# Decode's products in float32 on four column quarters, with three places for the raw weights and output tiles taken once

## The chip, the core and the metric

The kernel runs on one core of a Trainium2 chip. Its engines work at the same time and each in its own order: TensorE (PE, matrix products into PSUM; its weight loads are listed apart as PEld), VectorE (DVE), ScalarE (ACT), GpSimd (POOL) and SyncE (SP), whose queue here only starts transfers. Data are moved between device memory and the on-chip memory by 16 DMA engines, which are fed from queues of SP and of ACT. The metric is the device time of one execution in microseconds (us), the median of several; lower is better.

## The reference

One inference step of a hybrid decoder layer, for a prompt of 1024 tokens and for 8 samples of one token each, with the same weights, all in float32:

```python
x = layer_norm(ALPHA * x + 0.5 * swiglu(x, ffn1_wi, ffn1_wo), ...)
z = x @ w_in + b_in                    # q, k, v, o, i, f, B, C, h, merge gates a and b
h, C, n, m = mlstm_chunkwise(q, k, v, log_i, log_f, C0, n0, m0)
y_a = (head_norm(h) * sigmoid(z_o)) @ w_a
y_b = (z_B * short_conv(z_C * z_h)) @ w_b
x = layer_norm(ALPHA * x + (sigmoid(z_ga) * y_a + sigmoid(z_gb) * y_b) @ w_mix)
x = layer_norm(ALPHA * x + 0.5 * swiglu(x, ffn2_wi, ffn2_wo), ...)
x = layer_norm(ALPHA * x + sigmoid(x @ w_pg) * (p @ w_pp), ...)
```

For a sample, one step of the mLSTM, for each of 4 heads and 8 samples, is an update of a 256 x 256 state matrix and one product with the query:

```python
C_new = w_c * C + outer(k * exp(dec - m_new), v)
num = C_new^T q          # then divided by the normaliser and normed over the head
```

In the kernel this part is called decode: 32 matrices, each read from `state_C`, changed, multiplied with the query and written to `C_sample`.

## The kernel before

**Precision.** A large product in float32 is made from products in a reduced format (`float32r`): each operand is split into a high part (ACT copies and rounds it) and a low part (DVE subtracts), and three products, high x high, high x low, low x high, are added in PSUM. The helpers are `hilo` (L210 to L212), `put` within `wcomb` (L258, L259) for weights, and `product` (L429 to L434).

**Pairs.** The projection `z = x @ w_in` is worked in pairs of 128 columns (256 columns at once) by a scheme with seven products instead of eight (`pair`, L438 and after). A pair has 14 steps: seven combinations j of weights and inputs, each for two groups of tokens s (256 and 260 columns). A step is 4 x 3 matmuls. Snapshots of partial sums go to on-chip memory by ACT (L450, L457, L461, L465), and DVE adds them into the output tiles (L454, L469, L470, L474).

**Weights.** For a pair, `wraw` loads two halves of 512 KB each (L245, SP's queue) into two places and `wcomb` makes seven weight combinations from both: L267 (DVE) and L270 (DVE), L268 and L275 (POOL) are sums and differences. The combinations go to a ring of nine slots, so the preparation of the next pair runs while the present pair computes.

**The last twelve pairs.** `lin` (L1018 and after) is called twelve times: four pairs for the gate o (stored in blocks, `oscr`), four for the merge gate b (`bscr`) and four for a (`ascr`). ACT applies the sigmoid (L1025); SP's queue starts the stores (L949 for o, L1027 for a and b). In these twelve pairs `count["step"]` is 0: each pair takes its raw weights in the same two places, `praws[2:4]`, and makes its two output tiles anew on the same two places `psgs[0:2]`. The other places of both lists serve decode.

**Decode beside the pairs.** `beside` is a list of lists: after each step of a pair its first entry is taken off and what it holds is recorded at that point, behind the latest snapshot on ACT. 168 entries are made for the 168 steps of the twelve pairs. For matrix n, counted from step 9n/2: `dec_load` (transfer on ACT's queue, step +0), `dec_value` (the value row to all partitions, +4), `dec_update` (+7: ACT scales the matrix, L1187; DVE adds the outer product, L1189), `dec_split` for both halves of 128 rows (+7 and +9: `hilo`, and after the second half the store to `C_sample`), and `dec_product` for both halves (+12 and +14, L1203). A product has the query of one sample as stationary operand: 16 columns, the high and the low part of the query, each with zeros but in the sample's column, so the products of the 8 samples of a head add up in one PSUM bank `pn` (16 rows). After the last one DVE copies the bank (L1207), `dec_sum` adds high and low parts by a small matmul with `sel` (L1211), and `dec_norm` and `dec_end` finish the head. Three places hold matrices, two hold value rows, three hold split halves.

**Order.** The tile framework sets the semaphores and plans the order on each engine with a cost model; a tile that is made anew on a place waits until all accesses to the old one are over, and within one tile overlapping accesses are ordered. Each engine, and each transfer queue, takes its instructions in the planned order.

Of the kernel before, what the change touches and what calls it, by code (L numbers as in the profile page):

```python
# [9 lines left out]
R = mybir.dt.float32r  # L10
I32 = mybir.dt.int32
AF = mybir.ActivationFunctionType
OP = mybir.AluOpType
# [23 lines left out]
def F_(ap):  # L37
    return ap.bitcast(F32)
# [25 lines left out]
def layer_kernel(ctx: ExitStack, tc: tile.TileContext, I, O):  # L64
    nc = tc.nc
    V, S, G, T, DQ = nc.vector, nc.scalar, nc.gpsimd, nc.tensor, nc.sync
# [10 lines left out]
    def gen(i, dt=F32, n=NT):  # L77

        tag = f"a{i}" if isinstance(i, int) else i
        return sb.tile([128, 1024 if tag in WN else 4 * BM], dt, name=tag, tag=tag)[:, :1024 if tag in WN else n]  # L80
# [14 lines left out]
    def tmp(n=BM):  # L95
        return tmpp.tile([128, BM], F32, name="tmp", tag="tmp")[:, :n]
# [17 lines left out]
    ident = sb.tile([128, 128], F32, name="ident")  # L114
# [17 lines left out]
    def slot():  # L132
        s = ring["slots"][ring["i"] % len(ring["slots"])]
        ring["i"] += 1
        return gen(s, R)
# [27 lines left out]
    def wrow(w, rows, half, dst=None):  # L163

        t = [wload(w[r:r + 128, half * 512:(half + 1) * 512].rearrange("p (k n) -> p k n", n=128), 4, 128,
                   gen(dst[i], R) if dst else None) for i, r in enumerate(rows)]
        return [[(hi[:, j, :], lo[:, j, :]) for hi, lo in t] for j in range(4)]
# [42 lines left out]
    def hilo(dst, src):  # L210
        order_["hi"] = S.copy(dst[0], src).ins
        order_["lo"] = V.tensor_tensor(dst[1], src, F_(dst[0]), op=OP.subtract).ins  # L212
# [28 lines left out]
    def wraw(w, c0, slots):  # L241
        out = []
        for i in range(2):
            t = gen(slots[i])[:, :D].rearrange("p (k n) -> p k n", n=256)
            DQ.dma_start(t, w[i * 512:(i + 1) * 512, c0:c0 + 256].rearrange("(k p) n -> p k n", p=128))  # L245
            out.append(t)
        return out

    def wcomb(raws):

        lo_, up = raws
        g = lo_.shape[1]
        a11, a21, a12, a22 = lo_[:, :, 0:128], lo_[:, :, 128:256], up[:, :, 0:128], up[:, :, 128:256]

        def put(src):
            s = slot()
            hi, lo = (s[:, i * 512:i * 512 + g * 128].rearrange("p (k n) -> p k n", n=128) for i in range(2))
            S.copy(hi, src)  # L258
            V.tensor_tensor(lo, src, F_(hi), op=OP.subtract)  # L259
            return hi, lo  # L260

        def fresh():
            return rawp.tile([128, 512], F32, name="raw", tag="raw")[:, :g * 128].rearrange("p (k n) -> p k n", n=128)

        s1, s2, s3 = fresh(), fresh(), fresh()
        out = [put(a11)]
        V.tensor_tensor(s1, a21, a22, op=OP.add)  # L267
        G.tensor_tensor(s3, a11, a21, op=OP.subtract)  # L268
        out.append(put(a12))
        V.tensor_tensor(s2, s1, a11, op=OP.subtract)  # L270
        out.append(put(s2))
        out.append(put(a22))
        out.append(put(s1))
        s4 = fresh()
        G.tensor_tensor(s4, a12, s2, op=OP.subtract)  # L275
        out.append(put(s3))
        out.append(put(s4))
        return out
# [157 lines left out]
    beside = []  # L436
# [299 lines left out]
    w_in = I["w_in"][0]  # L736
    XP = x7()
    praws, psgs = [31, 32, 24, 25], [22, 23, 20, 21]
# [8 lines left out]
    vscr = tc.dram_tile([4, 8, 256], F32, name="vscr")  # L747
    count = {"sg": 0, "w": 0, "step": 1}

    def sg_pair():  # L750
        i = 2 * (count["sg"] % 2)
        count["sg"] += count["step"]
        return [gen(psgs[i + q]) for q in range(2)]

    def in_pair(c0):
        i = 2 * (count["w"] % 2)
        count["w"] += count["step"]
        return wcomb(wraw(w_in, c0, praws[i:i + 2]))


    nT = sb.tile([128, 2, 32], F32, name="nT")
# [22 lines left out]
    def sg(shape, name):  # L784
        return sb.tile(shape, F32, name=name)
# [192 lines left out]
    for m in range(8):  # L978
        DQ.dma_start(x2scr[m], rp[m])
    w0 = in_pair(CC0)  # L980
    for k in range(2):
        lin_store((qscr, kscr)[k], qk[k], 0, k)
# [140 lines left out]
    sgn = sg([8, 258], "sgn")  # L1123
    dn = sg([8, 4], "dn")
    dec = {}
    sel = sg([16, 8], "sel")
    PS = sb.tile([128, 128], R, name="ps_")

    def smp_load(i, t):
        DQ.dma_start(t[:, 0:64].rearrange("p (m b) -> p m b", b=8), smscr[i].rearrange("m p b -> p m b"))  # L1130
        return t[:, 0:64].rearrange("p (h t b) -> p h t b", h=4, t=2)
# [19 lines left out]
        V.tensor_copy(dn, pd[0:8, 0:4])  # L1151

    def dec_start():
        t = gen(psgs[2], R)
        dec["qd"] = [t[:, i * 256:i * 256 + 256].rearrange("p (t a b) -> p t a b", t=2, b=16) for i in range(2)]
        c0, c1 = gen(psgs[3]), gen(praws[1])
        dec["cd"] = [c0[:, 0:512], c0[:, 512:1024], c1[:, 0:512]]
        dec["vb"] = [c1[:, 512:768], c1[:, 768:1024]]
        u = gen(praws[0], R)
        dec["hl"] = [v.rearrange("p (i e) -> p i e", i=2) for v in (t[:, 512:1024], u[:, 0:512], u[:, 512:1024])]  # L1160
        q8 = smp_load(0, tmp())
        dec["q"] = [PS[:, 64 * i:64 * i + 64].rearrange("p (h t b) -> p h t b", h=4, t=2) for i in range(2)]
        hilo(dec["q"], q8)
        V.tensor_tensor(sel, ident[0:16, 0:8], ident[0:16, 8:16], op=OP.add)

    def dec_query(h):
        e8 = eye8.rearrange("p (a b) -> p a b", b=8)
        for dt in range(2):
            for i in range(2):
                x = F_(dec["q"][i][:, h, dt])  # L1170
                V.tensor_tensor(dec["qd"][h % 2][:, dt, :, 8 * i:8 * i + 8], x[:, None, :].to_broadcast([128, 8, 8]), e8,
                                op=OP.mult)

    def dec_load(n):
        h, s = divmod(n, 8)
        dec[n] = dec["cd"][n % 3].rearrange("p (t e) -> p t e", t=2)
        S.dma_start(dec[n], I["state_C"][0, s, h].rearrange("(t p) e -> p t e", p=128))
        if s == 0:
            dec_query(h)

    def dec_value(n):
        S.dma_start(dec["vb"][n % 2], bass.AP(tensor=vscr.tensor, offset=vscr.offset + n * 256, ap=[[0, 128], [1, 256]]))
# [5 lines left out]
        for dt in range(2):  # L1188
            V.scalar_tensor_tensor(cd[:, dt], vb, kws[:, h, dt, s:s + 1], cd[:, dt], op0=OP.mult, op1=OP.add)  # L1189

    def dec_split(n, dt):
        h, s = divmod(n, 8)
        hl = dec["hl"][(2 * n + dt) % 3]
        hilo((hl[:, 0], hl[:, 1]), dec[n][:, dt])
        if dt:
            S.dma_start(O["C_sample"][0, s, h].rearrange("(t p) e -> p t e", p=128), dec[n])

    def dec_product(n, dt):
        h, s = divmod(n, 8)
        if s + dt == 0:  # L1200
            dec["pn"] = psp.tile([128, 512], F32, name="pn", tag="pn", bufs=1)
        for i in range(2):
            T.matmul(dec["pn"][0:16, 0:256], dec["qd"][h % 2][:, dt, s], dec["hl"][(2 * n + dt) % 3][:, i],  # L1203
                     start=(s + dt + i == 0), stop=(s == 7 and dt == 1 and i == 1))
        if s + dt == 8:
            dec["both"] = tmp(256)[0:16]
            V.tensor_copy(dec["both"], dec["pn"][0:16, 0:256])  # L1207

    def dec_sum(h):
        ph = aux(256)  # L1210
# [32 lines left out]

    if count["sg"] % 2:
        psgs = psgs[2:] + psgs[:2]
    count.update(sg=0, w=1, step=0)
    dec_start()
    beside += [[] for _ in range(168)]
    for n in range(32):
        for f, late in ((dec_load, 0), (dec_value, 4), (dec_update, 7)):  # L1250
            beside[n * 9 // 2 + late].append(partial(f, n))
        for dt in range(2):
            beside[n * 9 // 2 + 7 + 2 * dt].append(partial(dec_split, n, dt))
            beside[n * 9 // 2 + 12 + 2 * dt].append(partial(dec_product, n, dt))
        if n % 8 == 7:
            for f, late in ((dec_sum, 20), (dec_norm, 23), (dec_end, 28)):
                beside[n * 9 // 2 + late].append(partial(f, n // 8))
# [27 lines left out]
    for i in (34, 29, 20, 21):  # L1285
        t = gen(i, R, 4 * BM).rearrange("p (i t e) -> p i t e", i=2, e=BM)[:, :, :, 0:258]
# [126 lines left out]
    def wa_in(t, m):  # L1413
        s = gen((18, 28, 23)[m % 3]).rearrange("p (d n) -> p d n", n=516)
        DQ.dma_start(s[:, 0], ascr[m][:, half_cols(t)])
        DQ.dma_start(s[:, 1], tbscr[m][:, half_cols(t)])
        return s, wcol(I["w_a"][0], m * 128)
# [60 lines left out]
    for m in range(0, 8, 2):  # L1478
        u = [wa_in(1, m + i) for i in range(2)]
# [17 lines left out]
    w = wrow(w_mix, rows, 0, r_[0:5] + [18])  # L1497
# [167 lines left out]
    def out_new(t=None):  # L1665
        k = count["o"]
        count["o"] += 1
        return obufs[k % 2] if t is None else t, wkb.rearrange("p a b c -> p (a b c)")[:, k % 2 * 28:k % 2 * 28 + 28]
# [109 lines left out]
    t = gen(21, R)  # L1778
# [14 lines left out]
    o, st = [t[:, 520:1032] for t in (a31, a32)], out_new()[1]  # L1793
# [36 lines left out]
```

## Time and profile before

| | |
|---|---|
| time, median of 3 runs | 2691.32 us (2690.53 to 2692.86) |
| the profiled execution | 2685.85 us, span 2684.0 us |
| matmul records of decode's products (L1203) | 128, from 1236.2 to 1457.7 us |
| small products of `dec_sum` (L1211) | 8 records, from 1294.8 to 1466.5 us |
| weight load of 16 columns for L1203 | 94 ns median |
| scaling of a state matrix on ACT (L1187) | 32 of 810 to 839 ns |
| DMA in the last twelve pairs (1220 to 1478 us) | 202 GB/s |
| DVE and ACT over the whole span | 70% and 48% busy |

A line of the profile has the engine, the line of the kernel, the operation, what it writes and reads by the program's names, sizes, and times. Matmul records overlap: one of 260 columns is listed with about 0.28 us, but the next one starts 0.12 us later; the distance of the starts is what a matmul costs PE. In a list of waits the three numbers are us in total, times, and the longest. A row of a window has its start and end, its length, and then the busy time and the count of PE, PEld, DVE, ACT and POOL, the granted clock of PE, the busy share of the DMA engines and GB/s. In brackets at the end of a timeline row stands the idle time before it and what ended it.

### The profile page before, as it was taken

Reading aid. Unit: us, or ns where it says so; the run is one execution under the profiler, and the core shown is the slowest. Engines: PE = TensorE matmul, PEld = TensorE weight load, DVE = VectorE, ACT = ScalarE, POOL = GpSimd, SP = SyncE. Lnnn points to the kernel's source line nnn. Section 1 sums busy time; section 2 is a strip of 40 time slices with the busy share of each in tenths; the row PEclk is TensorE's granted clock in tenths of the full one; section 3 lists DMA queues with packets and bytes.
Section 4 is the critical chain, followed back from the end, with each engine's and each line's share of the span. In section 5 each row is a group of like instructions: output and inputs, shape, how many; then the busy total and the mean of one; then the engine's idle time right before and its main releaser. Section 6 shows DMA issues by size and latency. Waiting matters only on the chain.

```text
span 2684.0 us, 56381 instructions
## 1 busy us (share of the span) xinstructions
PE 2638.3 (98%) x21775; PEld 2604.1 (97%) x21775; DVE 1871.4 (70%) x4124; ACT 1287.8 (48%) x2839; POOL 652.8 (24%) x648
## 2 busy tenths in 40 slices
PE   9999999999999999999999999999999999999998
PEld 9999999999999999999999999999999999999887
DVE  6755556997885756656666678658855555888887
ACT  5444446433554445446666555425544444543351
POOL 2222221112421111111111345323422222111454
PEclk9999999999999999999999999999999999999999
DMA  6333235432332434236657776821423323643211
GB/s 207 103 108 107 91 105 197 161 121 68 115 97 88 123 99 127 79 89 191 188 176 243 236 238 219 256 81 46 157 91 107 104 89 107 219 154 114 86 47 58
DMA packets 311924, 355.15 MB, mean 132 GB/s; under 512 B 28536, under 2 KB 246344, under 8 KB 311656
## 3 DMA queue, kind: packets, MB, share of 16 engines
q1 hardware_dynamic: 289336, 330.30, 38.7%
q10 hardware_dynamic: 22320, 21.26, 2.6%
q8 instruction: 170, 2.79, 0.4%
q14 instruction: 98, 0.80, 0.1%
HBM read 246.09 MB, written 105.42 MB: 131 GB/s over the span
## 4 chain that ended last, share of the span: by engine, by line
PE 79%; DVE 9%; DMA 5%; ACT 2%; issue 2%; POOL 1%; SPq 0%; ACTq 0%; DVEq 0%; POOLq 0%
PE mm L432 13%; PE mm L433 13%; PE mm L434 13%; PE aux L432 5%; PE aux L434 5%; PE aux L433 5%; PE mm L172 5%; PE mm L174 5%; PE mm L173 5%; PE pn L172 1%; PE pn L173 1%; PE pn L174 1%; DVE a L212 1%; DVE a L589 1%; DVE w L259 1%
## 5 line engine op out<-in xcount | busy, mean ns | idle before, releaser
L432 PE MATMUL mm<-a,w 128*128 128x260 f32 (+1 forms) x2313 | 654.9, 283 | 3.4 <-DVE a L612 2.5
L433 PE MATMUL mm<-a,w 128*128 128x260 f32 (+1 forms) x2313 | 651.0, 282 | 0.9 <-DVE a L212 0.9
L434 PE MATMUL mm<-a,w 128*128 128x260 f32 (+1 forms) x2313 | 649.9, 281 | 0.0
L432 PEld LDWEIGHTS mm<-a,w 128*128 128x128 f32 x2313 | 435.3, 188 | 9.0 <-issue 3.7
L433 PEld LDWEIGHTS mm<-a,w 128*128 128x128 f32 x2313 | 435.7, 188 | 1.5 <-DVE a L212 1.3
L434 PEld LDWEIGHTS mm<-a,w 128*128 128x128 f32 x2313 | 435.3, 188 | 0.1
L275 POOL TENSOR_TENSOR raw<-a,raw 128x512 f32<-128x512 f32 (+2 forms) x98 | 124.6, 1272 | 1149.1 <-issue 448.8
L259 DVE TENSOR_TENSOR w<-raw,w 128x512 fp32r<-128x512 f32 (+2 forms) x258 | 174.6, 678 | 189.5 <-ACT w L258 188.2
L432 PE MATMUL aux<-a,w 128*128 128x260 f32 (+1 forms) x1000 | 282.0, 282 | 1.8 <-DVE a L454 1.5
L433 PE MATMUL aux<-a,w 128*128 128x260 f32 (+1 forms) x1000 | 281.1, 281 | 0.0
L434 PE MATMUL aux<-a,w 128*128 128x260 f32 (+1 forms) x1000 | 281.1, 281 | 0.0
L432 PE MATMUL mm<-a,e 128*128 128x260 f32 (+1 forms) x785 | 222.5, 283 | 0.9 <-DVE a L612 0.6
L433 PE MATMUL mm<-a,e 128*128 128x260 f32 (+1 forms) x785 | 221.2, 282 | 0.7 <-DVE a L212 0.7
L434 PE MATMUL mm<-a,e 128*128 128x260 f32 (+1 forms) x785 | 220.8, 281 | 0.0
L174 PE MATMUL mm<-a,w 128*128 128x256 f32 (+3 forms) x739 | 208.0, 284 | 0.2 <-DVE w L149 0.2
L172 PE MATMUL mm<-a,w 128*128 128x260 f32 (+4 forms) x695 | 198.0, 286 | 3.2 <-DVE a L647 1.7
L173 PE MATMUL mm<-a,w 128*128 128x260 f32 (+4 forms) x695 | 197.0, 285 | 0.0
L258 ACT CAST w<-a 128x512 fp32r<-128x512 f32 (+2 forms) x200 | 117.2, 587 | 161.5 <-PE mm L434 95.3
L432 PEld LDWEIGHTS aux<-a,w 128*128 128x128 f32 x1000 | 188.2, 188 | 2.9 <-DVE a L454 2.0
L434 PEld LDWEIGHTS aux<-a,w 128*128 128x128 f32 x1000 | 188.2, 188 | 0.0
L433 PEld LDWEIGHTS aux<-a,w 128*128 128x128 f32 x1000 | 188.2, 188 | 0.0
L258 ACT CAST w<-raw 128x512 fp32r<-128x512 f32 (+2 forms) x258 | 152.2, 591 | 65.6 <-PE aux L434 21.6
(546 smaller groups left out, 7726.1 us busy)
## 6 DMA issues: line engine op xcount, KB each, us to landing
a<-in_ffn_wi_dram SPq DMA_DIRECT2D x80, 512.0 KB
a<-in_w_in_dram SPq DMA_DIRECT2D x68, 512.0 KB
a<-hsum SPq DMA_DIRECT2D x119, 258.0 KB
hsum<-a SPq DMA_DIRECT2D x68, 258.0 KB
a<-in_ffn_wo_dram SPq DMA_DIRECT2D x40, 384.0 KB
a<-in_state_C_dram ACTq DMA_DIRECT2D x32, 256.0 KB
out_dram<-a ACTq DMA_DIRECT2D x32, 256.0 KB
raw<-in_w_b_dram SPq DMA_DIRECT2D x32, 256.0 KB
```

The source lines that it names most:

```text
L172: T.matmul(ps, wh, xh, start=(i == 0), stop=False)
L173: T.matmul(ps, wh, xl, start=False, stop=False)
L174: last = T.matmul(ps, wl, xh, start=False, stop=(i == n - 1))
L212: order_["lo"] = V.tensor_tensor(dst[1], src, F_(dst[0]), op=OP.subtract).ins
L258: S.copy(hi, src)
L259: V.tensor_tensor(lo, src, F_(hi), op=OP.subtract)
L275: G.tensor_tensor(s4, a12, s2, op=OP.subtract)
L432: T.matmul(ps, wh, xh, start=start and kp == 0, stop=False, skip_group_check=True)
L433: T.matmul(ps, wh, xl, start=False, stop=False, skip_group_check=True)
L434: T.matmul(ps, wl, xh, start=False, stop=stop and kp == len(xs) - 1, skip_group_check=True)
L589: V.tensor_tensor(lo, F_(lo), F_(hi), op=OP.subtract)
```

## The change

Decode's products are made in float32, without a split: `dec_split` and its `hilo` are gone, and `dec_store` only stores. Products come for two matrices at once (after odd n): four matmuls, for two samples and two halves of rows, each into its own quarter of the columns of the array (`tile_position=(0, 32 * j)`) and so into its own 32 rows of `pn`. The stationary operand has 32 columns per sample, of which 8 are used and the rest is zero from a memset. `pn` is copied with all 128 rows, and `sel` adds the four quarters. Four places hold state matrices. The value row is loaded two steps earlier, the store stands at +10, the product at +10 counted from the odd matrix. The two output tiles are made once for all twelve pairs (`fixed`), and the raw weights rotate over three places `praws[1:4]`; `praws[0]` holds the value rows and the stationary operand.

```diff
+    fixed = []
+
     def sg_pair():
+        if count["step"] == 0:
+            return fixed
         i = 2 * (count["sg"] % 2)
-        count["sg"] += count["step"]
+        count["sg"] += 1
         return [gen(psgs[i + q]) for q in range(2)]

     def in_pair(c0):
-        i = 2 * (count["w"] % 2)
-        count["w"] += count["step"]
-        return wcomb(wraw(w_in, c0, praws[i:i + 2]))
+        i = count["w"]
+        count["w"] += 1
+        return wcomb(wraw(w_in, c0, [praws[1 + (2 * i + q) % 3] for q in range(2)] if count["step"] == 0 else
+                          praws[i % 2 * 2:i % 2 * 2 + 2]))
...
     def dec_start():
...
+        c0, c1, c2 = gen(psgs[2]), gen(psgs[3]), gen(praws[0])
+        dec["cd"] = [c[:, o:o + 512] for c in (c0, c1) for o in (0, 512)]
+        dec["vb"] = [c2[:, 0:256], c2[:, 256:512]]
+        dec["qd"] = c2[:, 512:1024].rearrange("p (t a b) -> p t a b", t=2, b=32)
+        G.memset(dec["qd"], 0.0)
+        q8 = smp_load(0, F_(PS))
+        V.tensor_tensor(sel, ident[:, 0:8], ident[:, 32:40], op=OP.add)
+        for j in (64, 96):
+            V.tensor_tensor(sel, sel, ident[:, j:j + 8], op=OP.add)
+        dec["q"] = q8

     def dec_query(h):
         e8 = eye8.rearrange("p (a b) -> p a b", b=8)
         for dt in range(2):
-            for i in range(2):
-                x = F_(dec["q"][i][:, h, dt])
-                V.tensor_tensor(dec["qd"][h % 2][:, dt, :, 8 * i:8 * i + 8], x[:, None, :].to_broadcast([128, 8, 8]), e8,
-                                op=OP.mult)
+            V.tensor_tensor(dec["qd"][:, dt, :, 0:8], dec["q"][:, h, dt][:, None, :].to_broadcast([128, 8, 8]), e8,
+                            op=OP.mult)
...
-    def dec_split(n, dt):
+    def dec_store(n):
         h, s = divmod(n, 8)
-        hl = dec["hl"][(2 * n + dt) % 3]
-        hilo((hl[:, 0], hl[:, 1]), dec[n][:, dt])
-        if dt:
-            S.dma_start(O["C_sample"][0, s, h].rearrange("(t p) e -> p t e", p=128), dec[n])
-
-    def dec_product(n, dt):
+        S.dma_start(O["C_sample"][0, s, h].rearrange("(t p) e -> p t e", p=128), dec[n])
+
+    def dec_product(n):
         h, s = divmod(n, 8)
-        if s + dt == 0:
+        if s == 0:
             dec["pn"] = psp.tile([128, 512], F32, name="pn", tag="pn", bufs=1)
         for i in range(2):
-            T.matmul(dec["pn"][0:16, 0:256], dec["qd"][h % 2][:, dt, s], dec["hl"][(2 * n + dt) % 3][:, i],
-                     start=(s + dt + i == 0), stop=(s == 7 and dt == 1 and i == 1))
-        if s + dt == 8:
-            dec["both"] = tmp(256)[0:16]
-            V.tensor_copy(dec["both"], dec["pn"][0:16, 0:256])
+            for dt in range(2):
+                j = 2 * i + dt
+                T.matmul(dec["pn"][32 * j:32 * j + 32, 0:256], dec["qd"][:, dt, s + i], dec[n + i][:, dt],
+                         start=(s == 0), stop=(s == 6), tile_position=(0, 32 * j), skip_group_check=True)
+        if s == 6:
+            dec["both"] = tmp(256)
+            V.tensor_copy(dec["both"], dec["pn"][:, 0:256])
...
-    count.update(sg=0, w=1, step=0)
+    fixed.extend(gen(psgs[q]) for q in range(2))
+    count.update(w=0, step=0)
     dec_start()
     beside += [[] for _ in range(168)]
     for n in range(32):
-        for f, late in ((dec_load, 0), (dec_value, 4), (dec_update, 7)):
+        for f, late in ((dec_load, 0), (dec_value, 2), (dec_update, 7), (dec_store, 10)):
             beside[n * 9 // 2 + late].append(partial(f, n))
-        for dt in range(2):
-            beside[n * 9 // 2 + 7 + 2 * dt].append(partial(dec_split, n, dt))
-            beside[n * 9 // 2 + 12 + 2 * dt].append(partial(dec_product, n, dt))
+        if n % 2:
+            beside[n * 9 // 2 + 10].append(partial(dec_product, n - 1))
+        if n % 8 == 0:
+            beside[n * 9 // 2 + 8].append(partial(dec_query, n // 8))
```

More of the change, by code (lines that the diff above doesn't have):

```diff
@@ L1125, in layer_kernel @@
     dec = {}
-    sel = sg([16, 8], "sel")
+    sel = sg([128, 8], "sel")
     PS = sb.tile([128, 128], R, name="ps_")
@@ L1153, in dec_start @@
     def dec_start():
[L1154 to L1164, printed above, removed]
+        c0, c1, c2 = gen(psgs[2]), gen(psgs[3]), gen(praws[0])
[8 more added lines that the diff above has]
+        dec["q"] = q8
     def dec_query(h):
@@ L1168, in dec_query @@
         for dt in range(2):
-            for i in range(2):
-                x = F_(dec["q"][i][:, h, dt])
-                V.tensor_tensor(dec["qd"][h % 2][:, dt, :, 8 * i:8 * i + 8], x[:, None, :].to_broadcast([128, 8, 8]), e8,
-                                op=OP.mult)
+            V.tensor_tensor(dec["qd"][:, dt, :, 0:8], dec["q"][:, h, dt][:, None, :].to_broadcast([128, 8, 8]), e8,
+                            op=OP.mult)
     def dec_load(n):
         h, s = divmod(n, 8)
-        dec[n] = dec["cd"][n % 3].rearrange("p (t e) -> p t e", t=2)
+        dec[n] = dec["cd"][n % 4].rearrange("p (t e) -> p t e", t=2)
         S.dma_start(dec[n], I["state_C"][0, s, h].rearrange("(t p) e -> p t e", p=128))
-        if s == 0:
-            dec_query(h)
     def dec_value(n):
```

## The prediction

> **What bounds the kernel now.** I read the page's head first, then the chain that ended last, then one window over the stage that the change touches, from the first to the last of the twelve pairs that have decode beside them.
>
> ```profile
> span 2684.0 us, 56381 instructions
> PE 2638.3 (98%) x21775; PEld 2604.1 (97%) x21775; DVE 1871.4 (70%) x4124; ACT 1287.8 (48%) x2839; POOL 652.8 (24%) x648
> ...
> PE 79%; DVE 9%; DMA 5%; ACT 2%; issue 2%; POOL 1%; SPq 0%; ACTq 0%; DVEq 0%; POOLq 0%
> ```
>
> ```profile
> 1220.00:1478.50 258.50, 252.22 (x2078) 243.54 (x2076) 172.20 (x408) 166.34 (x379) 31.27 (x25) 1.00 0.67 202
> 1240.00:1260.00 20.00, 20.00 (x171) 19.77 (x170) 16.00 (x33) 13.73 (x32) 2.70 (x2) 1.00 0.79 215
> ```
>
> TensorE (PE) bounds the whole and this stage too; its clock is full (1.00). A full 20 us holds 171 matmuls, 0.117 us each, so a step (12 matmuls) lasts 1.4 us. The 2078 records of the stage would fill 243 us of the 258.5: at most 15 us are lost, and that still holds restarts, a few slower float32 products and missing records. DVE stands at 67% and ACT at 64%: neither is the bound, but both work in order, so a wait at their head can reach PE. The waits of PE in this stage, and of DVE:
>
> ```profile
> PE pn L1203 <- DVE tmp L1207: 1.8, 1, 1.8
> PE aux L432 <- DVE a L454: 1.8, 3, 1.1
> PE pn L1203 <- DVE a L212: 0.9, 1, 0.9
> PE mm L432 <- DVE a L470: 0.8, 3, 0.4
> PE aux L432 <- DVE tmp L212: 0.6, 1, 0.6
> PE pn L1203 <- ACT a L211: 0.3, 1, 0.3
> ```
>
> ```profile
> DVE raw L267 <- DMA a<-in_w_in_dram: 11.7, 7, 2.6
> DVE a L1189 <- DMA a<-vscr: 11.0, 6, 3.7
> ...
> DVE a L454 <- DMA bscr<-a: 5.9, 3, 3.3
> DVE a L454 <- DMA oscr<-a: 5.7, 2, 3.1
> ...
> DVE a L454 <- DMA sm<-st: 3.8, 1, 3.8
> DVE a L454 <- DMA ascr<-a: 3.1, 2, 1.9
> ```
>
> PE always waits for a DVE or ACT result, but DVE itself waits for transfers: raw weights (L267), the value row of decode (L1189), and the store that still reads the output tile (L454). The largest PE wait shows the link: an addition held up by a transfer, and the copy of decode's sum (L1207) queued behind it, for which PE waits 1.8 us.
>
> ```profile
> 1287.47 0.42 DVE L454 TENSOR_TENSOR a<-sreg,aux 128x256 f32<-128x256 f32 x1 [3.84 <-DMA sm<-st]
> ...
> 1289.41 0.41 DVE L1207 COPY tmp<-pn 16x256 f32<-16x256 f32 x1
> ```
>
> A wait costs PE more than its listed length:
>
> ```profile
> 1226.46 0.28 PE L432 MATMUL mm<-a,e 128*128 128x260 f32 x1
> 1227.81 0.39 PE L432 MATMUL aux<-a,w 128*128 128x260 f32 x1 [1.07 <-DVE a L454]
> 1228.04 0.29 PE L433 MATMUL aux<-a,w 128*128 128x260 f32 x1
> ```
>
> From 1226.46 to 1228.04 stand 1.58 us for two matmuls that need 0.24: 1.34 lost, 0.27 more than listed.
>
> **The change, part by part.**
>
> **Waits.** Output tiles taken once: now every pair takes its two tiles anew and its first addition waits for all readers of the old ones, stores included; with the tile kept, only readers of the same columns count, and block 0's store is the oldest. Raw weights over three places: a pair's second half can be loaded when the previous pair's first half has been read, about half a preparation earlier than now. The value row is asked for five steps ahead of its use (late 2 against 7) instead of three: 7.1 us instead of 4.3, so of the six waits only the 3.7 keeps a remainder (0.9). Decode's matrices get four places instead of three. So the causes of five rows of PE's list go; they are 1.8+1.8+0.9+0.8+0.3 = 5.6 us in nine waits, with 9 x 0.27 = 2.4 of restarts 8.0 us. The sixth (0.6, behind the value transposes of the pair before) stays. What else could be late: the product now comes three steps (4.3 us) after the update of its second matrix, the update takes 0.8 us on ACT and two DVE operations, and PE's whole queue of pair matmuls stands behind a late product; the store issue on ACT also follows the update by three steps, with the casts of the weights behind it. I take 85% of 8.0, **-6.8 us**; bounds 0 (the same lateness moved) and -8.0.
>
> **Casts.** The hi/lo splits of 64 half matrices go:
>
> ```profile
> L212 DVE TENSOR_TENSOR a<-a,a 128x256 fp32r<-128x256 f32 (+1 forms) x72 | 36.6, 521 | 5.9 <-ACT a L211 5.7
> L211 ACT CAST a<-a 128x256 fp32r<-128x256 f32 (+1 forms) x72 | 30.7, 430 | 23.7 <-DVE a L1189 21.7 <-DMA a<-yscr 0.9 <-PE pn L1203 0.6
> ```
>
> 64 of 72 are decode's: 27 us of ACT and 33 of DVE within 258. They lie beside PE, so they count nothing themselves; they are a reason to believe that the waits go. The new extras are small and beside PE too: one POOL memset (POOL is busy 31 of 258.5 us), two more additions for `sel`, and half as many query multiplications. Traffic is the same: each state matrix, value row and weight is moved once, as now; only the issue places change. SP's queue:
>
> ```profile
> SPq L245 <- POOL raw L275: 30.0, 9, 4.7
> ```
>
> A weight load waiting for its place blocks the output stores behind it; a third place shortens that.
>
> **Products.** This is the large unknown. Now there are 128 reduced-precision products of 16 columns (32 matrices, two halves of rows, two parts each), of which this row groups 84:
>
> ```profile
> L1203 PE MATMUL pn<-a,a x84: 275/279/290, 1239.2 to 1454.6; 128*16 128x256 f32 x84
> ```
>
> ```profile
> 1412.89 0.40 PE L1203 MATMUL pn<-a,a 128*16 128x256 f32 x2
> 1413.13 0.28 PE L432 MATMUL mm<-a,w 128*128 128x260 f32 x1
> ```
>
> Two take 0.24 us, 0.12 each, without any gap around them: 128 x 0.12 = 15.4 us. Afterwards there are 64 float32 products in 16 groups of four. Float32 products of the same length exist:
>
> ```profile
> 2523.21 0.28 PE L172 MATMUL mm<-a,w 128*128 128x256 f32 x1
> 2523.33 0.59 PE L407 MATMUL aux<-sreg,onesm 128*128 128x256 f32 x2
> 2523.57 0.47 PE L173 MATMUL mm<-a,w 128*128 128x256 f32 x1
> 2523.87 0.28 PE L174 MATMUL mm<-a,w 128*128 128x256 f32 x1
> ```
>
> ```profile
> 1294.60 0.28 PE L434 MATMUL mm<-a,w 128*128 128x260 f32 x1
> 1294.81 0.59 PE L1211 MATMUL aux<-tmp,sel 16*8 16x256 f32 x2
> 1295.33 0.39 PE L432 MATMUL mm<-a,w 128*128 128x256 f32 x1
> 1295.56 0.28 PE L433 MATMUL mm<-a,w 128*128 128x256 f32 x1
> ```
>
> One float32 matmul of the program is two records (two halves). From 2523.21 to 2523.87 are 0.66 us with two ordinary matmuls, which leaves 0.42, 0.21 a half. With a small stationary operand (L1211) the same sum gives 0.96 - 0.24 = 0.72: 0.30 more, as gaps before, after and one matmul later. I charge these 0.30 to a group as the price of going to a part of the array and back. What four quarters do side by side no row shows. Bounds: all eight halves one behind the other, 8 x 0.21 + 0.30 = 1.98 us a group, 31.7 in all, +16.3; or the four quarters wholly side by side, 2 x 0.21 + 0.30 = 0.72, 11.5 in all, -3.9. Every record of this trace starts in program order, and the two halves of a quarter are neighbours in it; the second half must follow the first in the same quarter, and the next quarter's first half can start only beside it. That makes five slots, 5 x 0.21 + 0.30 = 1.35 us, 21.6 in all, **+6.2 us**. It is also the middle of the bounds (2, 5, 8), so I take it, although the nearest rows (halves of undivided products, one behind the other) lean to eight.
>
> The Trainium skill, "TensorE: Matmul & The Clock Gate", Part 3, says that matmuls on different quarters overlap but start and end strictly in program order, and gives 2.38 times for three column tiles. The order agrees with the starts here; no run before the change shows the overlap. An estimate from that factor (3.2 for four quarters) would make a group 1.68 / 3.2 + 0.30 = 0.83 us and the sum -2.2 instead of +6.2. The skill's "TensorEngine Tiling (Array Packing)", Key Properties, speaks against the change: every change of tiling mode drains the engine. The gaps around L1211 agree; without any such charge (16 x 0.30 = 4.8) the sum would be +1.4 instead of +6.2.
>
> The sum: +6.2 - 6.8 = -0.6 us, against the profiled execution's 2685.85 us (span 2684.0 plus 1.85 around it). The median of the runs is 2691.32, 5.5 us above this execution; I put the difference on the median: **2690.7 us**.
>
> **Rivals.**
>
> *Quarters wholly side by side* (both halves of each run in its quarter without holding up the next): -3.9 - 6.8 = -10.7, 2680.6 us, faster. For it: the quarters share neither columns nor output partitions. Against it: the program order of the halves. The Trainium skill's "TensorEngine Tiling (Array Packing)", Key Properties, says that tiles run independently, which would give this case.
>
> *One behind the other* (slower): the place is the group of L1203's successor, eight halves of 0.21 us with PE's queue behind them: +16.3 - 6.8 = +9.5, 2700.8 us. For it: all float32 rows here follow one another. It decides from 16 groups costing more than 15.4 + 6.8 + 5.4 = 27.6 us, 1.73 us each. Faster would need under 15.4 + 6.8 - 5.4 = 16.8, 1.05 each.
>
> *The waits stay* (the kept tile still waits as a whole, or a product waits for its update in place of the waits removed), with five slots: only a third of 8.0 goes, +6.2 - 2.7 = +3.5, 2694.8 us. For it: the shorter way from update to product, and a DVE that was up to 3.8 us late; against it: DVE and ACT lose work and each cause is met by a place more.
>
> **How the numbers follow.** About 0.2%, 5.4 us, is what a measurement of this kernel can tell from no change. Five slots with waits gone 0.45 (of it 0.08 faster, 0.35 same, 0.02 slower, by 3 us either way for the order that the planner makes anew); side by side 0.22, faster; one behind the other 0.18 (0.16 slower, 0.02 same); waits stay 0.15 (0.08 same, 0.07 slower). Together faster 0.30, same 0.45, slower 0.25. The range reaches to both other cases, 2679 to 2702: outside it lie parts of "side by side" with all waits gone and of "one behind the other" with few gone (down to 16.3 above the median with none), some 0.16. The forecast alone would be 2686 to 2695.
>
> **What would show it.** The eight records of a group and the start of the pair matmul after the next: 1.35 us longer than without the group says five slots, 0.72 side by side, 1.98 in a row. DVE's waits on transfers at L454 and at the weight sum should fall from 18.5 and 11.7 us to under 5 together, that on the value row to about 1; PE's list should keep the 0.6 and under 1.5 more. A PE wait of the new product for the update would show the third rival. I would be wrong also if the planner, which orders anew with other costs, put work of the next stage differently, or if the clock fell below 1.00 in the groups.

## The result, and the profile after

The changed kernel takes 2675.08 us in the median (2672.63 to 2676.36, 4 runs) against 2692.09 us for the kernel before beside it (2690.53 to 2694.49): ratio 0.9935, interval 0.9918 to 0.9952. The forecast was 2690.7 us with a range of 2679 to 2702: the time lies below it. In later jobs the ratio was 0.9942 (0.9929 to 0.9955) and 0.9948 (0.9934 to 0.9962). The changed kernel stays within 2672 and 2678 us in all of them; the kernel before moves between 2682 and 2699 from one execution and one job to another.

The head of the page after, and the chain that ended last:

```profile
span 2674.6 us, 56234 instructions
...
PE 2635.3 (99%) x21775; PEld 2597.2 (97%) x21775; DVE 1840.7 (69%) x4053; ACT 1272.1 (48%) x2774; POOL 650.9 (24%) x649
...
PE 85%; DVE 7%; DMA 4%; issue 2%; ACT 2%; POOL 1%; SPq 0%; DVEq 0%; ACTq 0%; POOLq 0%
```

PE is as busy as before in a shorter span, and the share of DVE and DMA in the chain fell from 14% to 11%. Where the time went is read best between two products that both kernels have, one before the first of the twelve pairs (`dec_dot`) and one behind the last (keys and queries of chunk 0). These rows give their first and last starts, first in the kernel before:

```profile
L1150 PE MATMUL aux<-ones,cbuf x16: 163/163/170, 1199.9 to 1200.3; 128*8 128x1 f32 x16
...
L1319 PE MATMUL aux<-a,a x128: 272/275/377, 1478.8 to 1687.4; 128*128 128x128 f32 x128
```

and after:

```profile
L1155 PE MATMUL aux<-ones,cbuf x16: 163/163/170, 1203.0 to 1203.4; 128*8 128x1 f32 x16
...
L1320 PE MATMUL aux<-a,a x128: 272/275/377, 1470.2 to 1678.9; 128*128 128x128 f32 x128
```

From the first start of the one to the first start of the other (called the stage below) 278.9 us became 267.2: 11.7 less. Behind it the products of L1319 and L1320 take 208.6 and 208.7 us, and ahead of it PE has the same matmuls in the same order in both. They took 3.1 us longer in this profile of the changed kernel (1199.9 to 1203.0), so the span fell by only 9.4 us, from 2684.0 to 2674.6, while the stage fell by 11.7. Three profiles of the kernel before give 278.9, 281.3 and 275.8 us for the stage, three of the changed one 267.2, 267.2 and 267.1.

All that is left of PE's waits after the change, and then of DVE's waits for transfers at the three lines of the prediction, both from 1220 to 1478.5 us:

```profile
PE mm L172 <- ACT w L1333: 0.2, 1, 0.2
```

```profile
DVE a L1189 <- DMA a<-vscr: 2.5, 4, 1.4
```

PE waits for nothing of the twelve pairs any more. At the weight sum (L267) and at the additions (L454) no wait for a transfer is left; the value row keeps 2.5 us, where the prediction had about 1. One group of float32 products, then the records of the same group that run between 1248.79 and 1248.84 us, and those that run between 1249.25 and 1249.35:

```profile
1248.58 0.28 PE L434 MATMUL mm<-a,w 128*128 128x260 f32 x1
1248.79 0.64 PE L1202 MATMUL pn<-a,a 128*32 128x256 f32 x8
1249.36 0.39 PE L432 MATMUL mm<-a,w 128*128 128x256 f32 x1
1249.58 0.28 PE L433 MATMUL mm<-a,w 128*128 128x256 f32 x1
```

```profile
1248.79 0.42 PE L1202 MATMUL pn<-a,a 128*32 128x256 f32 x4
```

```profile
1249.03 0.40 PE L1202 MATMUL pn<-a,a 128*32 128x256 f32 x4
```

By 1248.84 four of the eight records have begun, 50 ns after the first; the other four begin together from 1249.03, 0.24 us after the first. The trace has a sign of which they are: the semaphore increments that `one_quarter` below has on its second and fourth record, the second halves of its first two products, stand here on the fifth and sixth. So the first halves of the four products start first and then the second halves. The eight are through, to the next start, in 0.57 us, where the two halves of a single L1211 took 0.52. By the sum of the prediction the group costs 1.00 (from 1248.58 to 1249.58) - 0.24 = 0.76 us: the four quarters run side by side.

### The profile page after: what moved, and what is told of

Its sections match the earlier page's. It is cut to its first block, busy times and chain, and to the rows that moved or that the text cites. A ratio compares the mean times of both kernels' runs of the same rounds, so it can differ in the third digit from the quotient of the medians.

```text
span 2674.6 us, 56234 instructions
## 1 busy us (share of the span) xinstructions
PE 2635.3 (99%) x21775; PEld 2597.2 (97%) x21775; DVE 1840.7 (69%) x4053; ACT 1272.1 (48%) x2774; POOL 650.9 (24%) x649
## 4 chain that ended last, share of the span: by engine, by line
PE 85%; DVE 7%; DMA 4%; issue 2%; ACT 2%; POOL 1%; SPq 0%; DVEq 0%; ACTq 0%; POOLq 0%
PE mm L432 15%; PE mm L433 14%; PE mm L434 14%; PE aux L432 6%; PE aux L434 6%; PE aux L433 6%; PE mm L172 5%; PE mm L174 5%; PE mm L173 5%; PE pn L172 1%; PE pn L174 1%; PE pn L173 1%; DVE a L212 1%; DVE a L589 1%; DVE a L612 1%
```

## The experiments

**Both kernels again, the parts, and the whole.** `before_again` and `before_third` are the kernel before, `after_again` and `after_third` the changed one, without an edit. The three edits on waits can each be undone alone:

```diff
 # A: output tiles made anew
-            return fixed
+            return [gen(psgs[q]) for q in range(2)]
 # B: raw weights in two places
-        return wcomb(wraw(w_in, c0, [praws[1 + (2 * i + q) % 3] for q in range(2)] if count["step"] == 0 else
+        return wcomb(wraw(w_in, c0, praws[2:4] if count["step"] == 0 else
 # C: value row three steps ahead instead of five
-        for f, late in ((dec_load, 0), (dec_value, 2), (dec_update, 7), (dec_store, 10)):
+        for f, late in ((dec_load, 0), (dec_value, 4), (dec_update, 7), (dec_store, 10)):
```

`products_alone` is the changed kernel with A, B and C; `kept_tiles_alone` is the kernel before with `fixed` taken over from the change.

> The unchanged kernel of before, for its profile on the chip on which the others run. Stage: from the products of dec_dot to the first product of keys and queries of chunk 0; 278.9 us before, 267.2 after the change, 11.7 less, while the medians differ by 17. Theory 1 (the stage is all that the change touches): the stage is again 277 to 281 us, and what is over 11.7 us lies outside the stage and is the difference of two executions. Theory 2 (the first profile of before was a lucky one): the stage itself is 283 us or more, with more waits of PE in it. Ratio 1.000 +- 0.002.

> The changed kernel once more, beside the kernel before on the same chip. Theory 1: stage 266 to 269 us, everything outside it as in the kernel before of the same chip within 2 us, ratio 0.9945 to 0.996 (11.7 us and a bit). Theory 2: ratio 0.993 to 0.994 again (17 us) because before loses more in the stage than its first profile showed.

> The changed kernel with the three edits on waits undone: output tiles made anew, raw weights in the same two places each pair, the value row at +4. Float32 quarters, no splits and four places for matrices remain. Theory 1 (products are worth 3 us, waits are cured by the kept tiles, the third place and the earlier value row): 16 groups of 0.76 us, stage 273 to 276 us, ratio 0.998 to 0.999, DVE still waits 10 us or more for transfers at L454. Theory 2 (the work taken from ACT and DVE is what cured the waits): stage 267 to 270 us, ratio 0.994 to 0.996, no wait of PE in the stage.

> The kernel before with one edit: the two output tiles are made once for the twelve pairs. Theory 1: DVE's waits for stores at L454 (18.5 us) go, with them PE's waits on L454 and on L1207 (3.6 us listed, 4.7 with restarts): stage 273 to 276 us, ratio 0.998 to 0.999. Theory 2 (cast work is what delays): the waits move to the weight sum and the value row, stage 277 to 280 us, ratio 0.9995 to 1.0005.

Measured: `before_again` 0.9999 (0.999 to 1.0009), stage 281.3 us; `after_again` 0.9942 (0.9929 to 0.9955), stage 267.2; `products_alone` 1.000 (0.9991 to 1.001), stage 280.6; `kept_tiles_alone` 0.997 (0.9959 to 0.9981), stage 273.5. The first two lie between theories 1 and 2, so they don't decide. The third is met by neither theory: the new products with less work on DVE and ACT are worth nothing without the edits on waits. Kept tiles alone, without the products, are worth 8 us in the medians and 5 in the stage (from 278.7, the mean of the three profiles of before). In `products_alone` PE waits as in the kernel before, and also at the new product, for the update just ahead of it (and then DVE's longest wait):

```profile
PE mm L432 <- DVE a L470: 3.4, 4, 1.9
PE pn L1202 <- DVE a L1189: 2.3, 3, 1.5
PE aux L432 <- DVE a L454: 1.2, 2, 0.7
```

```profile
DVE raw L267 <- DMA a<-in_w_in_dram: 28.8, 8, 5.7
```

In `before_again` the longest wait shows what such a wait costs beyond its length. The timeline of PE, and windows of 4 us (behind the busy times: granted clock, DMA share, GB/s):

```profile
1311.44 0.39 PE L1203 MATMUL pn<-a,a 128*16 128x256 f32 x2
1313.64 0.38 PE L432 MATMUL aux<-a,e 128*128 128x256 f32 x1 [1.81 <-DVE a L454]
...
1314.45 0.42 PE L434 MATMUL aux<-a,e 128*128 128x256 f32 x1
1314.66 0.41 PE L432 MATMUL aux<-a,e 128*128 128x256 f32 x1
```

```profile
1312.00:1316.00 4.00, 2.36 (x13) 2.36 (x14) 2.80 (x10) 2.22 (x6) 0.00 (x0) 0.77 0.15 42
1316.00:1320.00 4.00, 4.00 (x29) 3.95 (x29) 2.34 (x7) 2.47 (x8) 1.36 (x1) 0.80 0.49 122
1320.00:1324.00 4.00, 4.00 (x36) 3.95 (x35) 2.09 (x5) 2.77 (x6) 1.29 (x1) 1.00 0.77 240
```

Soon after the wait the matmuls start 0.21 us apart instead of 0.12 and the granted clock falls. From 1314.10 to 1317.45, 16 matmuls took 3.35 us instead of 1.9: 1.4 us on top of the wait. The wait of the same length in the first profile (1.80 us at 1289.97) was not followed by this, so one and the same wait costs 2.0 or 3.4 us. The 280.6 us of `products_alone` hold such a stretch too, after its wait of 1.9 us at L470:

```profile
1256.00:1260.00 4.00, 3.67 (x19) 3.67 (x20) 3.42 (x8) 3.10 (x7) 0.00 (x0) 0.63 0.46 131
```

**The law of the quarters.**

```diff
-                T.matmul(dec["pn"][32 * j:32 * j + 32, 0:256], dec["qd"][:, dt, s + i], dec[n + i][:, dt],
-                         start=(s == 0), stop=(s == 6), tile_position=(0, 32 * j), skip_group_check=True)
+                k = j % 1        # two_quarters: j % 2
+                T.matmul(dec["pn"][32 * k:32 * k + 32, 0:256], dec["qd"][:, dt, s + i], dec[n + i][:, dt],
+                         start=(s == 0 and j < 1), stop=(s == 6 and j >= 3), tile_position=(0, 32 * k), ...)
```

> The changed kernel with all four float32 products of a group in the first quarter of the columns, one sum instead of four; everything else as changed. Law A (each quarter works for itself, a group costs its fullest quarter's halves x 0.21 us and 0.34 for going there and back): 8 x 0.21 + 0.34 = 2.02 us a group against 0.76, 16 x 1.26 = 20.2 us more, stage 287 us, some 2697 us, ratio 1.002. Law B (halves overlap only with the next product, in program order): the same 2.02 here, as nothing can overlap. If the time grows by less than 15 us, float32 halves in one quarter overlap too, and the quarters are not the reason.

> The changed kernel with the four products of a group in two quarters, in turn (0, 1, 0, 1). Law A: 4 x 0.21 + 0.34 = 1.18 us a group, 16 x 0.42 = 6.7 us more than changed, stage 274 us, ratio 0.9967. Law B: five slots, 5 x 0.21 + 0.34 = 1.39 us, 10.1 us more, stage 277 us, ratio 0.998.

A group of `one_quarter`, then one of `two_quarters`:

```profile
1247.21 0.28 PE L434 MATMUL mm<-a,w 128*128 128x260 f32 x1
1247.43 1.91 PE L1203 MATMUL pn<-a,a 128*32 128x256 f32 x8
1249.27 0.39 PE L432 MATMUL mm<-a,w 128*128 128x256 f32 x1
1249.50 0.28 PE L433 MATMUL mm<-a,w 128*128 128x256 f32 x1
```

```profile
1248.12 0.28 PE L434 MATMUL mm<-a,w 128*128 128x260 f32 x1
1248.33 1.06 PE L1203 MATMUL pn<-a,a 128*32 128x256 f32 x8
1249.32 0.39 PE L432 MATMUL mm<-a,w 128*128 128x256 f32 x1
1249.54 0.27 PE L433 MATMUL mm<-a,w 128*128 128x256 f32 x1
```

2.29 - 0.24 = 2.05 us and 1.42 - 0.24 = 1.18 us a group (law A: 2.02 and 1.18); stages 286.9 and 273.7 us (expected 287 and 274); ratios 1.0014 (1.0005 to 1.0023) and 0.9962 (0.995 to 0.9975). So law A, with the 0.34 from the group of the changed kernel, holds for two other placements: a group costs the halves of its fullest quarter, 0.21 us each, and 0.34 for going there and back. Five slots (1.39 us with two quarters) don't fit.

**One cure taken away.** `fresh_tiles` is the change with A, `two_raw` with B, `value_late` with C.

> The changed kernel with one edit undone: the two output tiles are made anew for every pair. Theory 1 (each of the cures is needed): DVE waits again 12 to 20 us for stores at L454, PE waits behind it, stage 271 to 275 us, ratio 0.996 to 0.998, and the executions spread by 4 us or more. Theory 2 (with less work on DVE the waits find slack, and one cure among them is enough): stage 267 to 269 us, ratio 0.994 to 0.995.

> The changed kernel with one edit undone: raw weights in the same two places for each of the twelve pairs. Theory 1: DVE waits at the weight sum L267 for its transfer again, 10 to 29 us, with additions behind it that PE needs, stage 270 to 275 us, ratio 0.995 to 0.998. Theory 2: stage 267 to 269 us, as the weight sum has slack of its own, ratio 0.994 to 0.995.

> The changed kernel with one edit undone: the value row is asked for at +4 again, three steps ahead of its use. Taking back the kept tiles or the third place cost nothing, taking back all three cost all of the gain. Theory 3 (the value row is the one that counts): stage 277 to 281 us as with all three undone, ratio 0.998 to 1.000. Theory 4 (the cures stand in for one another: DVE has slack for one kind of wait, not for three): stage 267 to 270 us, ratio 0.993 to 0.995.

Measured: 0.9935 (0.9922 to 0.9947), 0.9935 (0.9922 to 0.9949) and 0.9945 (0.9931 to 0.9958). In the medians none of the three is needed when the other two are there, against theory 1. In the stage the third place still counts: 269.6 us without it, between the two theories, with a wait of 1.3 us of the product for its update. The other two stages are 267.5 and 268.0.

**Two cures taken away.** `only_value_lead` is the change with A and B, `only_third_place` with A and C, `only_kept_tiles` with B and C.

> The changed kernel with output tiles made anew and raw weights in two places; of the three edits on waits only the earlier value row remains. Theory 3: stage 267 to 270 us, ratio 0.993 to 0.995. Theory 4: two kinds of waits (stores 15 us, weights 12 us or more) meet on DVE, stage 272 to 278 us, ratio 0.996 to 0.999, with PE waits for L454 and L470.

> The changed kernel with output tiles made anew and the value row at +4; of the three edits only the third place for raw weights remains. Theory 3: stage 277 to 281 us, ratio 0.998 to 1.000. Theory 4: between one and three undone, stage 271 to 278 us, ratio 0.995 to 0.999.

> The changed kernel with raw weights in two places and the value row at +4; of the three edits only the kept output tiles remain. In the kernel before this edit alone gave 8 us (ratio 0.997). Theory 3: stage 277 to 281 us, ratio 0.998 to 1.000. Theory 4: stage 270 to 276 us, ratio 0.995 to 0.998.

Measured: 0.9987 (0.9977 to 0.9996), 0.995 (0.9937 to 0.9962) and 0.9958 (0.9946 to 0.9971). The earlier value row alone helps little; the third place or the kept tiles alone bring most, the third place more than either theory had (267.6 us against 271 or more). Beside the stages, the table has the sums of the rows of DVE that wait for transfers at L267, L1189 and L454, and of PE's rows that wait for DVE at the pairs and at decode's products, in the window of the twelve pairs:

| kernel | stage, us | DVE for transfers, us | PE, us |
|---|---|---|---|
| before, first profile | 278.9 | 43 | 5.9 |
| products_alone (none of the three) | 280.6 | 58 | 6.9 |
| only_value_lead | 280.6 | 52 | 6.2 |
| only_third_place | 267.6 | 38 | 1.5 |
| only_kept_tiles | 270.4 | 28 | 1.9 |
| value_late | 268.0 | 17 | 2.2 |
| fresh_tiles | 267.5 | 18 | 0 |
| two_raw | 269.6 | 16 | 1.5 |
| changed | 267.2 | 2.5 | 0 |

DVE can lose 18 us to transfers without PE waiting (`fresh_tiles`). In the three kernels where it loses more than 40, PE waits some 6 us or more. Below that the sum doesn't set the stage: 38 us go with 267.6 and 16 with 269.6, so it must matter which results the waits hold up. The effects of the three edits don't add; that they take from one slack of DVE fits, but no run shows the slack itself. The stages differ also by how often the planner interrupts the 16 groups of products with other matmuls: they run in 16 parts in `only_third_place` and `value_late`, in 18 in the changed kernel and `fresh_tiles`, in 19 in the other four with the new products, and each further part costs 0.7 us (below). In `only_value_lead` two waits (1.7 and 2.7 us) are followed by a clock of 0.58 and 0.57 in a window of 4 us, which is part of its 280.6.

**Casts back, cures without products, larger groups.** `casts_back` is `two_raw` with `dec_split` of the kernel before in the freed place, its results read by nothing; `kept_value` is `kept_tiles_alone` with the value row at +2; `groups_of_eight` takes four matrices at once:

```diff
 # casts_back
+            beside[n * 9 // 2 + 7 + 2 * dt].append(partial(dec_split, n, dt))
 # groups_of_eight, with B
-        dec["cd"] = [c[:, o:o + 512] for c in (c0, c1) for o in (0, 512)]
+        dec["cd"] = [c[:, o:o + 512] for c in (c0, c1, gen(praws[1])) for o in (0, 512)]
...
-        if n % 2:
-            beside[n * 9 // 2 + 10].append(partial(dec_product, n - 1))
+        if n % 4 == 3:
+            beside[n * 9 // 2 + 10].append(partial(dec_product, n - 3))
...
-            for f, late in ((dec_sum, 20), (dec_norm, 23), (dec_end, 28)):
+            for f, late in ((dec_sum, 19), (dec_norm, 23), (dec_end, 28)):
```

> The changed kernel with raw weights in two places (which alone gave 2675.2 us, stage 269.6 us) and, in the place so freed, the 64 splits of half matrices again, at +7 and +9 as in the kernel before; nothing reads their results. About 27 us more of ACT and 33 us of DVE (records overlap). Theory C (the casts filled the slack in which the transfers' waits now vanish): PE waits 3 us or more again, stage 273 to 279 us, ratio 0.996 to 0.999. Theory D (casts lie beside PE and cost nothing): stage 268 to 271 us, ratio 0.993 to 0.995.

> The kernel before with the output tiles kept and the value row at +2; products and splits as before. Kept tiles alone gave 8 us (stage 273.5 us). If the value row is a wait that matters beside casts: stage 270 to 272.5 us, ratio 0.995 to 0.9965. If not: stage 273 to 275 us, ratio 0.9965 to 0.998. In both cases the products are still 128 x 0.12 us, 3 us more than in four quarters.

> The changed kernel with raw weights in two places, six places for state matrices, products for four matrices at a time (eight float32 matmuls, two a quarter, 8 groups instead of 16) and the head's sum one step earlier, in the same step as a group. By the law of the quarters a group costs 4 x 0.21 + 0.34 = 1.18 us, 8 groups 9.4 us against 12.2, and four sums lose a going there and back: 3 to 4 us less than changed, stage 263 to 266 us, ratio 0.992 to 0.9935. If two raw places let PE wait for an update in the larger groups, the stage stays at 267 us or more.

> The unchanged kernel of before once more, for one more profile of its stage: two gave 278.9 and 281.3 us, the second with one stretch of lowered clock after a wait of PE of 1.8 us. If its executions spread because such waits come in different lengths, some with and some without a lowered clock, the stage is again another length, 278 to 286 us, and its excess over 278.9 is the length of the slow stretches and of longer waits.

> The changed kernel a third time, beside the kernel with cures alone. If the four quarters carry a part of their own (3 us): median 3 us under the other's, stage 267 us against 268.5. If the cures are all: the two medians within 1.5 us. Against the kernel before 0.994 to 0.9965: its time differs between the chips (2686 to 2692 us), the changed one's little.

> The kernel before with kept output tiles and the earlier value row once more, on the same chip as the changed kernel: stage 268 to 269.5 us, no wait of PE on DVE in it; median 2 to 4 us above the changed kernel's if the products count, within 1.5 us if not.

`casts_back`: 2675.9 us, stage 270.7 against 269.6 without the casts, as theory D has it. PE waits 0.4 us in the twelve pairs and 1.0 at the value transposes just ahead of them (L1043), not the 3 or more of theory C. Its ratio, 0.9961 (0.9949 to 0.9974), is in the range of theory C, but the kernel before ran at 2686.2 us there, 6 under the job of `two_raw`. Within about 1 us the casts lie beside PE. `kept_value`: 2677.1 and, on the chip of `after_third`, 2676.9 us (0.9959, 0.9946 to 0.9973), stage 268.5 and 268.7. Its one row of PE's waits in the twelve pairs, DVE's longest wait for a transfer there, and its products:

```profile
PE mm L172 <- ACT w L1337: 0.2, 1, 0.2
```

```profile
DVE raw L267 <- DMA a<-in_w_in_dram: 9.7, 6, 3.1
```

```profile
L1207 PE MATMUL pn<-a,a x84: 275/279/290, 1237.3 to 1446.0; 128*16 128x256 f32 x84
L1207 PE MATMUL pn<-a x44: 274/279/291, 1234.9 to 1449.1; 128*16 128x256 f32 x44
```

With the old products and casts, PE waits for nothing in the pairs. Two cures are worth 10 us of stage by themselves (278.7, the mean of three, to 268.6), and the stage is under both ranges expected of `kept_value`; against single profiles of before it is 7 to 13 us. The changed kernel on the same chip is at 2673.75 us (2672.97 to 2675.24) and 267.1: another 1.5 us of stage, 3.1 of the medians (their runs overlap in 2674.75 to 2675.24).

`groups_of_eight`: 2674.9 us, 0.9954 (0.9942 to 0.9967) against a kernel before that ran at 2686.2 us there. Its stage of 266.2 us is 1.0 under the changed kernel's, not 3 to 4. Waits are back (0.5 us at L1202, 0.2 at L470, 0.4 at the value transposes, L1043), which are a part of the shortfall; the rest stays open. Against `two_raw`, which has the same two places, it is 3.4. By its time it can't be told from the changed kernel; no version was found that clearly beats it. `before_third`: 2685.77 us, stage 275.8, under the expected 278 to 286, no lowered clock in the twelve pairs. So the kernel before has stages from 275.8 to 281.3 us in three profiles; that its slower executions lose still more in the same place fits, as the kernels with waits (before, `products_alone`, `only_value_lead`) spread over 8 to 11 us (11 to 24 executions) and most of the others over 2 to 6 (mostly 5 executions), but no profile of such an execution shows it. What is left of 15 us in the medians over 11.7 in the profiles stays open to that extent.

## Why the prediction was wrong, step by step

**What bounds the kernel** was right: PE, held up in this stage by DVE, and DVE by transfers.

**Products: the step that failed.** "The second half must follow the first in the same quarter, and the next quarter's first half can start only beside it. That makes five slots": +6.2 us. The reading that failed is that the two halves of a quarter are neighbours in the order of starts. The records show four first halves begun within 50 ns and the second halves 0.24 us later, and the quarter experiments give the fullest quarter's halves. This was the rival "wholly side by side", priced at 0.72 us a group and -3.9 (2680.6 us in all, still 5.5 above the measured time); a whole group takes 0.76. The going there and back, taken from L1211 as 0.30, was close: 0.34. But the planner split groups of the changed kernel, which no row of before could show:

```profile
1234.46 0.62 PE L1202 MATMUL pn<-a,a 128*32 128x256 f32 x2
1235.01 0.39 PE L432 MATMUL mm<-a,w 128*128 128x260 f32 x1
1235.24 0.28 PE L433 MATMUL mm<-a,w 128*128 128x260 f32 x1
1235.45 0.63 PE L1202 MATMUL pn<-a,a 128*32 128x256 f32 x6
```

Two records alone take as long as six or eight (0.55 and 0.56 us). That happened to two groups of 16, and it brings the products' own part near the 1.5 us of stage that lie between `kept_value` and the changed kernel: 16 x 0.76 and some 0.7 for each split are 13.6 us, against 15.4 for the old ones. The middle of far bounds was no ground for a forecast: -1.5 or so instead of +6.2 is 7.7 us, half of the 15.6 by which the forecast was off.

The Trainium skill, "TensorEngine Tiling (Array Packing)", Key Properties, says that tiles run independently, and so it is here, with both halves of a float32 product: 0.76 us for eight halves in four quarters against 2.05 in one. The strict program order that the Trainium skill's "TensorE: Matmul & The Clock Gate", Part 3, states did not bring the five slots that I drew from it; the profile has the starts of the halves, not their order in the program, so it does not speak against the order itself.

**Waits: right in kind, too small in size.** All the waits named went: 5.6 us listed to none. I took 85% of 8.0, -6.8; the two cures of `kept_value` gave -10.2 from the stage of the first profile (278.9 to 268.7), with products and casts untouched: 3.4 us of the error. (From the shortest stage of before, 275.8, it would be -7.1, so this size hangs on the profile.) The sixth wait of PE's list (0.6, at the value transposes) wasn't to go but went too, and the price of a wait had no room for the lowered clock, which makes a wait of 1.8 us cost 1.4 more in some executions. That a kernel with waits loses differently in each execution was no part of the sum: its median stood 5.5 us above the profiled execution, and "I put the difference on the median" carried this over to a kernel whose median is 1.3 us under its profiled execution and whose times spread by 4 us at most. That is most of the 4.5 us that are left of the error.

**Three cures** were added up as needed each; the table shows that the third place or the kept tiles would do. The **casts** cost about nothing, as said, but the waits go with the casts in place too (`kept_value`), so their going is not the reason that I had argued. The third place was to shorten SP's wait with stores behind it; it did not (30.0 before):

```profile
SPq L245 <- POOL raw L275: 34.5, 8, 5.7
```

What went is DVE's wait for the loads (28.8 us at L267 in `products_alone`, none in `only_third_place`), so it helps there, and not by a freer queue. **The waits stay**, the third rival, is what `products_alone` shows, with its new wait of the product for the update; in the change itself it doesn't appear.

## What to carry to other kernels

Small products that leave most of the columns idle can be put into quarters; the price is the fullest quarter's halves and one going there and back for each uninterrupted group, so a group that isn't split is cheaper. In this kernel that is so for float32 products of 256 columns. Price a wait on the bounding engine by what stands behind it in the executions, not by its listed length in one profile: take away the waits first, then look at what an operation costs. Cures of waits on one engine need not add up, so try each alone before building them all.

## What the runs showed of the hardware

In three profiles a pause of PE of 2.1 to 3.0 us between two starts was followed by a stretch of some 3.4 us in which matmuls start 0.21 instead of 0.12 us apart, and the granted clock of a 4 us window lies between 0.57 and 0.80. In others it was not: in the first profile of before a gap 1.96 us longer than the pitch (2.08 between the starts at 1287.89 and 1289.97) was followed by no lowered clock, nor was one of 2.45 us in `value_late` (from 1225.33 to 1227.78), while in `before_again` a gap as long as the first (1.96 us more than the pitch, from 1311.44 to 1313.64) was. What decides between the two stays open. The Trainium skill, "TensorE: Matmul & The Clock Gate", section "HAM oscillation", puts the limit for pauses at some 3.4 us; here shorter ones were enough, so the measurement decides.
